# A two-layer backbone in split float32: weight splits, transposes and PSUM tiles where one sub-layer hands over to the next

## The chip, the cores and the metric

The kernel runs on one core of one Trainium2 chip, in one launch. The metric is the device time of one execution, in microseconds (us). TensorE (PE) multiplies and transposes, VectorE (DVE) and ScalarE (ACT) work element by element, SyncE (SP) issues the transfers; SBUF and PSUM are the core's two memories.

## The reference, cut to what matters

One inference step of two layers with shared weights over 256 tokens (128 of a prompt, group 0; 128 of a sample, group 1), model width 2048. Each layer is a token-mixing sub-layer and a feed-forward sub-layer:

```python
shift1, scale1, gate1, shift2, scale2, gate2 = _modulation(cvec, p['w_mod'], p['b_mod'])
h = _rmsnorm(x, p['g_pre_mix']) * (1 + scale1) + shift1
au, av, q, k, v, ga, gb = jnp.split(h @ p['w_in'], SPLITS, axis=-1)
...
merged = jax.nn.sigmoid(ga) * (ya @ p['w_pa']) + jax.nn.sigmoid(gb) * (_merge_heads(yb) @ p['w_pb'])
x = x + gate1 * _rmsnorm(merged @ p['w_out'], p['g_post_mix'])
h = _rmsnorm(x, p['g_pre_ffn']) * (1 + scale2) + shift2
f = jnp.square(jax.nn.relu(h @ p['w_ff1'])) @ p['w_ff2']
x = x + gate2 * _rmsnorm(f, p['g_post_ffn'])
```

What matters here is the end of a sub-layer: the norm of a row of the output needs the whole row, the sum `x + gate * norm` needs that norm, the next norm needs the whole new row, and only then can the next sub-layer's projection of that token begin.

## The kernel before

**Precision.** Every projection is done as three matmuls on pairs of high and low parts, `high*high + high*low + low*high`. A weight tile `raw` (128 x 1024, 512 KB, one transfer) is split by `split`: ACT copies it to the rounded `wh`, DVE subtracts `wl = raw - wh`. Activations are split in the same way into two tiles (`hi`, `lo`, which the rows call `u`). There are 928 weight tiles.

**Order.** The program is written out by hand, instruction by instruction, and each engine runs its own instructions strictly in that order, waiting at each for what it needs. A list of items (weight tiles and small steps) is walked at the end of `body`; before each weight tile `advance` fetches, copies and subtracts as many further tiles as counters allow: `cap` limits how many split tiles may stand ready and not yet be used up, 4 in ordinary stretches.

**The handover.** A pass is one column block of 512 outputs with its 8 weight tiles; a pass over rows with tokens as outputs (`tok`) can be cut in two half passes, one for each group of tokens. At the end of a sub-layer `lay_halves` does this with the last pass and with the first pass of the next sub-layer. So PE does, in this order, 8 places for group 0 of the last pass, 8 for group 1 of the last pass, 8 for group 0 of the next first pass, and 8 for group 1. They are called here p0 to p7, q0 to q7, r0 to r7 and s0 to s7; a place is the six matmuls of one weight tile for one group. The 8 weight tiles of the last pass are held over p and q, the 8 of the next over r and s. There are three such handovers: mixing to feed-forward, feed-forward to mixing, and mixing to feed-forward again.

While q runs, group 0's rows go through `chain`: sum of the squares, square root (ACT) and reciprocal (DVE), the four residual sums (DVE) with their squares (ACT, the tile `dump`), again root and reciprocal; then, for each quarter o of the row, a scaling (`scaled`, DVE), four transposes on PE into the PSUM tile `aux`, scale and shift (on DVE for o = 0 and 2, on ACT for o = 1 and 3), the copy to `hi` (ACT), and the subtraction to `lo` (DVE). Quarter o serves the tiles 2o and 2o+1 of r. While r runs, the same is done for group 1, for s. `step` puts the stages of the chain at places: the stages are called at the numbers in `CHAIN_AT`, and the four transposes are the stages at 6, 7, 9 and 11. For group 0 these are ahead of q6, q7, r1 and r3, for group 1 ahead of r6, r7, s1 and s3. They are called T1 to T8 here. In a handover to a feed-forward sub-layer a ninth set (`turn`) follows at s5.

`ahead(p)` sets `cap` at each place from q0 on: 10 splits less those used up, plus `AHEAD`. With the numbers of before, ten tiles (the 8 of the last pass and two of the next) are split until q7; the splitting of the third tile of the next pass is released at r1, and stands in the queues of ACT and DVE behind what group 1's chain has put there at r0 and r1. `split` puts copy and subtraction out together.

**PSUM.** The pool `psm` has two tiles of 128 x 1024 (two banks each). A pass takes one; the two half passes of a pass write the two halves of the same one (`G.ps` is given up after the second), and what reads the finished first half (`out_stats`, or `post` of the next pass) stands as a wait for the second half's first matmul, since waits go by tiles.

Of the kernel before, what the change touches and what calls it, by code (L numbers as in the profile page):

```python
# [22 lines left out]
SPLIT_BUFS = 4  # L23
# [21 lines left out]
S_STEP = 4  # L45
MOD_ON_PE = [n in PE_QUADS for n in range(48)]
LAST = [11, 4, 11, 4]
CHAIN_AT = (0, 1, 3, 4, 6, 7, 9, 11, 12)
AHEAD = [0] * 9 + [1, 2, 3, 4, 5, 6] + [6] * 6 + [7, 8, 9]
SWAP16 = [i ^ 16 for i in range(32)]  # L50


# [38 lines left out]
def body(tc, io):  # L91
# [14 lines left out]
    def u4(dt=F32, name="u4"):  # L106
        return u4p.tile([128, 1024], dt, tag="u4", name=name)
# [10 lines left out]
    def v4(t, n=4):  # L118
        return t.rearrange("p (b t) -> p b t", b=n)

    def f(t):
        return t.bitcast(F32)
# [169 lines left out]
        while flush and todo:  # L292
            finish()

    def split(job):
        wh, wl = v4(u4(F32R, "wh"), 2), v4(u4(F32R, "wl"), 2)
        r = v4(job.raw, 2)
        act(wh, r, AF.Copy)
        tt(wl, r, f(wh), op=OP.subtract)
        job.parts = (wh, wl)  # L300

    def mm_half(job, gs=(0, 1)):
# [457 lines left out]
    def chain(Y, hs, nxt, spill, g):  # L760

        def rms(st):
            s = tiny(1)
            dve.tensor_reduce(s, st, axis=AX.X, op=OP.add)
            return rms_cols(s)

        r = rms(Y["st"][g])
        yield
        st = tiny(4)
        for o in range(4):  # L770
            x = X[o][:, g, :]
            dve.scalar_tensor_tensor(x, Y["y"][o][:, g, :], r, x, op0=OP.mult, op1=OP.add)
            if nxt is None:
                nc.sync.dma_start(io["y"][:, o, g], x)
                continue
            act(dump, x, AF.Square, accum_out=st[:, o:o + 1])
            if spill is not None:
                nc.sync.dma_start(spill[:, o, g], x)
        if nxt is None:
            return  # L780
        yield
        r2 = rms(st)
        yield
        ln, ma, mb = nxt
        w = slice(128 * g, 128 * g + 128)
        xr = {}

        def scaled(o):
            if o < 4:
                xr[o] = s2()  # L790
                dve.tensor_scalar(xr[o], X[o][:, g, :], r2, None, op0=OP.mult)

        scaled(0)
        yield
        last = None
        for o in range(4):
            if g == 0:
                hs.append(quad())
            scaled(o + 1)
            ps = aux()  # L800
            x = xr.pop(o)
            for b in range(4):
                nc.tensor.transpose(ps[:, 128 * b:128 * b + 128], x[:, 128 * b:128 * b + 128], ident)
            if last is not None:
                tt(*last, op=OP.subtract)
            t, ps = v4(s2()), v4(ps)
            if o % 2 == 0:
                for m, src, op in ((ma, ps, OP.mult), (mb, t, OP.add)):
                    mat(ln, m, 4 * o, g), mat(ln, m, 4 * o + 3, g)
                    tt(t, src, mv[:, ln, m, 4 * o:4 * o + 4, g:g + 1].to_broadcast([128, 4, 128]), op=op)  # L810
            else:
                for b in range(4):
                    act(t[:, b, :], ps[:, b, :], AF.Identity, scale=mat(ln, ma, 4 * o + b, g),
                        bias=mat(ln, mb, 4 * o + b, g))
            hi, lo = (h[:, :, w] for h in hs[o])
            act(hi, t, AF.Copy)
            last = lo, t, f(hi)
            yield
        tt(*last, op=OP.subtract)

# [49 lines left out]

    def held(on):
        def go():
            P["held"], P["cap"] = on, HELD if on else SPLIT_BUFS
        return go

    def ahead(p):

        P["cap"] = HELD - max(0, p if p < 8 else 8 if p < 16 else p - 8) + AHEAD[p]

    chains = [[], []]  # L880

# [103 lines left out]
    for i in range(1, 5):  # L985
# [19 lines left out]
        def second(p, a=args):  # L1005
            def go():
# [6 lines left out]
        items.append(to_end(ENDS[i], 8 * (24 if i == 2 else 30), i))  # L1013
        lay(seqs[i][0][1:-LAST[i]])

    P = dict(held=False, nl=0, nm=0, ns=0, live=0, mlive=0, sp=0, cap=0, md=0, t=0, free=False, ml=0.0, t0=0, m0=0, rate=0.0, s0=S_START,
             s=[(g, slice(k, k + 1024)) for g in range(2) for k in (0, 1024)], end=8 * ENDS[0])

    def fetch(j, name):
# [4 lines left out]
    def advance():  # L1024
        while True:
            moved = False
            if P["nm"] < min(len(mloads), P["end"]) and P["mlive"] < MOD_BUFS + (START_BUFS if P["nm"] < 64 else 0):
                fetch(mloads[P["nm"]], "mraw")
                P["mlive"] += 1
                P["nm"] += 1  # L1030
                moved = True
            if P["nl"] < len(loads) and P["live"] < (RAW_HELD if P["held"] else RAW_BUFS) and loads[P["nl"]].after <= P["nm"]:
                fetch(loads[P["nl"]], "raw")
                P["nl"] += 1
                P["live"] += 1
                moved = True
            if P["ns"] < P["nl"] and P["sp"] < P["cap"]:
                split(loads[P["ns"]])
                P["ns"] += 1
                P["sp"] += 1  # L1040
                P["live"] -= 1
                moved = True
            if not moved:
                return
# [16 lines left out]
    for it in items:  # L1061
        if callable(it):
            if not P["free"]:
                advance()
            it()
        elif isinstance(it, int):
            for _ in range(it):
                advance()
                one_mod()
        else:  # L1070
            advance()
            job, gs, last = it
            pump(bgm)
            if max(load.values()) < BG_LIMIT:
                pump(bg)
            mm_half(job, gs)
            P["sp"] -= last
            P["t"] += len(gs) / 2 if job.group.tok else 1
            spread_s()
            if P["free"] and P["md"] < min(P["nm"], P["end"], quota()) and P["t"] - mods[P["md"]][0].after >= MOD_AGE:  # L1080
                if not mods[P["md"]][1]:
                    if load["dve"] < P["ml"]:
                        one_mod()
                elif P["md"] + 1 < P["nm"] and P["t"] - mods[P["md"] + 1][0].after >= MOD_AGE:
                    one_mod()
                    one_mod()
            ease(len(gs) / 2)
            G = job.group
            if G.part and job.kh in (0, 1, 3, 5, 7):
                if job.kh == 0:  # L1090
                    G.acc = u4()
                    act(G.acc, G.ps, AF.Copy)
                else:
                    tt(G.acc, G.acc, G.ps, op=OP.add)
                G.ps = None
                if job.kh == 7:
                    G.post(*((G.acc, gs) if G.tok else (G.acc,)))
                    G.acc = None
            elif job.kh == G.n - 1:
                G.post(*((G.ps, gs) if G.tok else (G.ps,)))  # L1100
                if last:
                    G.ps = None

    ms.__exit__(None, None, None)
    for p in reversed(pools):
# [90 lines left out]
```

## Time and profile before

| | us |
|---|---|
| median of three runs (2846.80 to 2850.64) | 2846.85 |
| the profiled execution | 2849.79 |
| its span, first to last instruction | 2848.0 |
| PE busy in the span | 2772.1 (97%) |
| DVE busy | 2030.6 (71%) |
| ACT busy | 1285.3 (45%) |
| bytes moved | 722.56 MB, 254 GB/s on average |

The profile is of one execution, whose span lies 1.79 us under its own time and 1.15 us above the median of the runs. A row of the order of time begins with its start (us from the span's start) and its length, then engine, line, operation and tiles; a number in brackets is the time its engine sat idle before it, and what ended that. A matmul's end is modelled and lies after the start of the next, so idle time in brackets is a little shorter than the distance that the waiting matmul was pushed. Line 78 is the helper through which ACT and DVE work is recorded; lines 316 to 318 are the three matmuls of a place, line 803 the transposes of the chain.

### The profile page before, as it was taken

Reading aid. Unit: us, or ns where it says so; the run is one execution under the profiler, and the core shown is the slowest. Engines: PE = TensorE matmul, PEld = TensorE weight load, DVE = VectorE, ACT = ScalarE, POOL = GpSimd, SP = SyncE. Lnnn points to the kernel's source line nnn. Section 1 sums busy time; section 2 is a strip of 40 time slices with the busy share of each in tenths; the row PEclk is TensorE's granted clock in tenths of the full one; section 3 lists DMA queues with packets and bytes.
Section 4 is the critical chain, followed back from the end, with each engine's and each line's share of the span. In section 5 each row is a group of like instructions: output and inputs, shape, how many; then the busy total and the mean of one; then the engine's idle time right before and its main releaser. Section 6 shows DMA issues by size and latency. Waiting matters only on the chain.

```text
span 2848.0 us, 41915 instructions
## 1 busy us (share of the span) xinstructions
PE 2772.1 (97%) x16510; PEld 2385.9 (84%) x16510; DVE 2030.6 (71%) x2568; ACT 1285.3 (45%) x1596; POOL 0.7 (0%) x6
## 2 busy tenths in 40 slices
PE   7999999999899999999989999999989999999998
PEld 5788777777798989989869987788769899898997
DVE  4655767777688898897757888688766556656555
ACT  4344554334444444444544436544445444444443
POOL 0000000000000000000000000000000000000000
PEclk9999999999899999999999999999999999999999
DMA  9978778876578678787748677777736565756663
GB/s 383 369 260 312 281 255 295 278 274 260 185 266 304 243 277 300 253 299 251 246 177 302 243 272 248 261 269 283 293 132 246 204 215 200 255 186 215 216 204 137
DMA packets 204822, 722.56 MB, mean 254 GB/s; under 512 B 22993, under 2 KB 25681, under 8 KB 204625
## 3 DMA queue, kind: packets, MB, share of 16 engines
q1 hardware_dynamic: 204624, 719.89, 70.7%
q8 instruction: 129, 2.11, 0.3%
q14 instruction: 69, 0.56, 0.1%
HBM read 713.42 MB, written 6.37 MB: 253 GB/s over the span
## 4 chain that ended last, share of the span: by engine, by line
PE 94%; ACT 2%; DVE 2%; DMA 1%; issue 0%; SPq 0%; DVEq 0%; ACTq 0%
PE mm L316 19%; PE mm L317 18%; PE mm L318 18%; PE mm L325 11%; PE mm L326 11%; PE mm L327 11%; PE aux L236 2%; DMA mraw<-wm 1%; DVE wl L78 1%; ACT u L78 1%; ACT wh L78 1%; ACT s L78 1%; DVE u L78 0%; ACT dump L78 0%; DVE s L78 0%
## 5 line engine op out<-in xcount | busy, mean ns | idle before, releaser
L78 DVE TENSOR_TENSOR wl<-raw,wh 128x1024 fp32r<-128x1024 f32 x928 | 1108.0, 1221 | 373.9 <-ACT wh L78 355.4
L78 ACT ACTIVATE wh<-raw 128x1024 fp32r<-128x1024 f32 x928 | 949.1, 1055 | 651.5 <-PE mm L317 150.1
L316 PE MATMUL mm<-wh,u 128*128 128x512 f32 x2368 | 942.4, 398 | 37.8 <-ACT wh L78 27.8
L317 PE MATMUL mm<-wl,u 128*128 128x512 f32 x2368 | 929.6, 393 | 5.8 <-DVE wl L78 5.8
L318 PE MATMUL mm<-wh,u 128*128 128x512 f32 x2368 | 928.5, 392 | 2.4 <-DVE u L78 2.4
L325 PE MATMUL mm<-u,wh 128*128 128x256 f32 x2688 | 763.2, 284 | 0.0
L326 PE MATMUL mm<-u,wh 128*128 128x256 f32 x2688 | 760.6, 283 | 0.0
L327 PE MATMUL mm<-u,wl 128*128 128x256 f32 x2688 | 760.6, 283 | 0.0
L316 PEld LDWEIGHTS mm<-wh,u 128*128 128x128 f32 x2368 | 448.4, 189 | 158.9 <-ACT wh L78 37.9
L317 PEld LDWEIGHTS mm<-wl,u 128*128 128x128 f32 x2368 | 448.7, 189 | 98.5 <-DVE wl L78 9.9
L318 PEld LDWEIGHTS mm<-wh,u 128*128 128x128 f32 x2368 | 448.2, 189 | 98.8 <-DVE u L78 3.8
L325 PEld LDWEIGHTS mm<-u,wh 128*128 128x128 f32 x2688 | 515.8, 192 | 13.8 <-issue 10.5
L326 PEld LDWEIGHTS mm<-u,wh 128*128 128x128 f32 x2688 | 515.9, 192 | 0.4
L327 PEld LDWEIGHTS mm<-u,wl 128*128 128x128 f32 x2688 | 515.8, 192 | 0.0
L78 DVE SCALAR_TENSOR_TENSOR mraw<-mraw,sbc 128x1024 f32<-128x1024 f32 x248 | 303.8, 1225 | 8.8
L78 DVE SCALAR_TENSOR_TENSOR junk<-mraw,sbc 128x1024 bf16<-128x1024 f32 x248 | 301.9, 1217 | 8.3 <-DMA mraw<-wm 8.3
L78 ACT ACTIVATE u<-mm 128x1024 f32<-128x1024 f32 (+1 forms) x83 | 76.6, 933 | 429.7 <-PE mm L327 277.9
L78 DVE TENSOR_TENSOR u<-u,u 128x1024 fp32r<-128x1024 f32 (+4 forms) x74 | 72.9, 992 | 207.4 <-ACT u L78 206.9
L78 DVE TENSOR_TENSOR u<-u,mm 128x1024 f32<-128x1024 f32 (+1 forms) x60 | 64.1, 1076 | 103.4 <-PE mm L318 67.1
L78 ACT ACTIVATE u<-u 128x1024 f32<-128x1024 f32 (+3 forms) x86 | 81.4, 949 | 32.4 <-DVE u L78 27.2
L236 PE MATMUL aux<-mraw,csw 128*32 128x512 f32 (+1 forms) x608 | 76.0, 585 | 15.7 <-DMA mraw<-wm 15.6
L78 ACT ACTIVATE u<-aux 128x512 fp32r<-128x512 f32 (+2 forms) x48 | 23.6, 492 | 114.4 <-PE aux L607 68.7
(97 smaller groups left out, 660.2 us busy)
## 6 DMA issues: line engine op xcount, KB each, us to landing
raw<-f SPq DMA_DIRECT2D x512, 512.0 KB, 4.2
mraw<-wm SPq DMA_DIRECT2D x384, 512.0 KB, 5.2
raw<-wi SPq DMA_DIRECT2D x288, 512.0 KB, 4.5
raw<-wo SPq DMA_DIRECT2D x64, 512.0 KB, 6.8
raw<-pa SPq DMA_DIRECT2D x32, 512.0 KB, 4.4
raw<-pb SPq DMA_DIRECT2D x32, 512.0 KB, 4.4
u<-gd SPq DMA_DIRECT2D x32, 256.0 KB, 5.5
u<-xT SPq DMA_DIRECT2D x4, 512.0 KB, 5.7
```

Source lines behind the costliest of these rows:

```text
L78: return fn(out, *a, **k)
L236: nc.tensor.matmul(p[32 * c:32 * c + 32, :128 * nb], csw[:, kt, :], r[:, kt - k0, :], start=kt < 4, stop=kt > 11, skip_group_check=True, t ...
L316: nc.tensor.matmul(o, hh, wh[:, j, :], start=first, stop=False)
L317: nc.tensor.matmul(o, hh, wl[:, j, :], start=False, stop=False)
L318: nc.tensor.matmul(o, lo, wh[:, j, :], start=False, stop=last)
L325: nc.tensor.matmul(o, wh[:, j, s], hh, start=first and b % 2 == 0, stop=False, **kw)
L326: nc.tensor.matmul(o, wh[:, j, s], lo, start=False, stop=False, **kw)
L327: nc.tensor.matmul(o, wl[:, j, s], hh, start=False, stop=last, **kw)
```

## The change

Five edits, all at the handover.

1. `split` becomes `split_high` (the copy on ACT) and `split_low` (the subtraction on DVE), and `advance` releases them by two separate limits, `cap` and `low`. Outside the handover `low` is 99, so that a subtraction still follows its copy.
2. `AHEAD` holds a pair for each place, and the numbers differ: one more copy is released at q4, up to five more by r0; subtractions from q5 on, up to three more at q7.
3. The first transposes come one place sooner (5 in place of 6 in `CHAIN_AT`): T1 ahead of q5, T5 ahead of r5.
4. In the chain `scaled(o + 1)` is put out after the copy to `hi` and no longer ahead of the transposes of o, and for even o the subtraction to `lo` follows at once and not a stage later.
5. `G.ps` is given up after each half pass, so each takes its own PSUM tile, the two in turn.

```diff
-CHAIN_AT = (0, 1, 3, 4, 6, 7, 9, 11, 12)
-AHEAD = [0] * 9 + [1, 2, 3, 4, 5, 6] + [6] * 6 + [7, 8, 9]
+CHAIN_AT = (0, 1, 3, 4, 5, 7, 9, 11, 12)
+AHEAD = [(0, 0)] * 4 + [(1, 0), (2, 1), (3, 2), (3, 3), (5, 3), (5, 4), (5, 5), (5, 5)] + [(6, 6)] * 4 + [
+    (7, 7)] * 2 + [(8, 8)] * 2 + [(9, 9), (9, 9), (10, 10), (10, 10)]
...
-    def split(job):
-        wh, wl = v4(u4(F32R, "wh"), 2), v4(u4(F32R, "wl"), 2)
-        r = v4(job.raw, 2)
-        act(wh, r, AF.Copy)
-        tt(wl, r, f(wh), op=OP.subtract)
+    def split_high(job):
+        wh = v4(u4(F32R, "wh"), 2)
+        act(wh, v4(job.raw, 2), AF.Copy)
+        job.parts = (wh,)
+
+    def split_low(job):
+        wh, = job.parts
+        wl = v4(u4(F32R, "wl"), 2)
+        tt(wl, v4(job.raw, 2), f(wh), op=OP.subtract)
         job.parts = (wh, wl)
...
-            scaled(o + 1)
             ps = aux()
...
             act(hi, t, AF.Copy)
+            scaled(o + 1)
             last = lo, t, f(hi)
+            if o % 2 == 0:
+                tt(*last, op=OP.subtract)
+                last = None
             yield
...
-        P["cap"] = HELD - max(0, p if p < 8 else 8 if p < 16 else p - 8) + AHEAD[p]
+        own = HELD - max(0, p if p < 8 else 8 if p < 16 else p - 8)
+        P["cap"], P["low"] = own + AHEAD[p][0], own + AHEAD[p][1]
...
-            if P["ns"] < P["nl"] and P["sp"] < P["cap"]:
-                split(loads[P["ns"]])
+            if P["nh"] < P["nl"] and P["nh"] - P["done"] < P["cap"]:
+                split_high(loads[P["nh"]])
+                P["nh"] += 1
+                moved = True
+            if P["ns"] < P["nh"] and P["ns"] - P["done"] < P["low"]:
+                split_low(loads[P["ns"]])
                 P["ns"] += 1
-                P["sp"] += 1
...
                 G.post(*((G.ps, gs) if G.tok else (G.ps,)))
-                if last:
-                    G.ps = None
+                G.ps = None
```

ACT at the first handover, from group 0's second square root (ahead of T1) on, before. The tiles are `tiny` (a statistic), `u` and `s` (activations), `dump` (the squares), `wh` (a copied weight tile):

```order
L78 ACTIVATE tiny<-tiny,epsb 128x1
L78 ACTIVATE u_6106<-s_6115 128x4x128
L78 ACTIVATE s_6135<-aux,mv 128x128 x4
L78 ACTIVATE u_6125<-s_6135 128x4x128
L78 ACTIVATE dump,tiny<-mm 128x512
L78 ACTIVATE tiny<-tiny,epsb 128x1
L78 ACTIVATE u_6161<-s_6171 128x4x128
L78 ACTIVATE dump,tiny<-u_5620 128x512
L78 ACTIVATE dump,tiny<-u_5622 128x512
L78 ACTIVATE dump,tiny<-u_5624 128x512
L78 ACTIVATE dump,tiny<-u_5626 128x512
L78 ACTIVATE wh<-raw 128x1024 x2
```

The same place now:

```order
L79 ACTIVATE tiny<-tiny,epsb 128x1
L79 ACTIVATE wh<-raw 128x1024
L79 ACTIVATE u_6103<-s_6110 128x4x128
L79 ACTIVATE wh<-raw 128x1024 x2
L79 ACTIVATE s_6148<-aux,mv 128x128 x4
L79 ACTIVATE u_6141<-s_6148 128x4x128
L79 ACTIVATE dump,tiny<-mm 128x512
L79 ACTIVATE tiny<-tiny,epsb 128x1
L79 ACTIVATE wh<-raw 128x1024 x2
L79 ACTIVATE u_6184<-s_6192 128x4x128
L79 ACTIVATE dump,tiny<-u_5620 128x512
```

Five copies of weight tiles stand ahead of the squares of group 1's residual sums; none did.

DVE at the same handover, from group 0's fourth scaling on, before (`SCALAR_TENSOR_TENSOR` is group 1's residual sums):

```order
L78 TENSOR_SCALAR s_6163<-u_5626,tiny 128x512
L78 TENSOR_TENSOR u_6126<-s_6135,u_6125 128x4x128
L78 TENSOR_TENSOR s_6171<-aux,mv 128x512
L78 TENSOR_TENSOR s_6171<-s_6171,mv 128x512
L78 SCALAR_TENSOR_TENSOR u_5620<-u_5413,tiny,u_5620 128x512
L78 SCALAR_TENSOR_TENSOR u_5622<-u_5416,tiny,u_5622 128x512
L78 SCALAR_TENSOR_TENSOR u_5624<-u_5419,tiny,u_5624 128x512
L78 SCALAR_TENSOR_TENSOR u_5626<-u_5422,tiny,u_5626 128x512
L78 TENSOR_TENSOR wl<-raw,wh 128x1024 x2
L78 TENSOR_TENSOR u_6162<-s_6171,u_6161 128x4x128
L78 TENSOR_REDUCE tiny<-tiny 128x1
```

Now, from group 0's first `lo` on:

```order
L79 TENSOR_TENSOR u_6104<-s_6110,u_6103 128x4x128
L79 TENSOR_TENSOR wl<-raw,wh 128x1024 x2
L79 TENSOR_SCALAR s_6154<-u_5624,tiny 128x512
L79 TENSOR_TENSOR wl<-raw,wh 128x1024
L79 TENSOR_TENSOR u_5422<-mm,u_5422 128x512
L79 TENSOR_REDUCE tiny<-tiny 128x1
L79 RECIPROCAL tiny<-tiny 128x1
L79 TENSOR_TENSOR u_6142<-s_6148,u_6141 128x4x128
L79 TENSOR_TENSOR s_6192<-aux,mv 128x512
L79 TENSOR_TENSOR s_6192<-s_6192,mv 128x512
L79 TENSOR_SCALAR s_6196<-u_5626,tiny 128x512
L79 TENSOR_TENSOR u_6185<-s_6192,u_6184 128x4x128
```

Three subtractions of weight tiles now stand ahead of the reading of the last pass's second half (`u_5422<-mm`), with which group 1's chain begins; the second `lo` (`u_6142`) and the fourth scaling (`s_6196`) stand behind its first reciprocal.

PE where q begins, before and now, with the numbers of the tiles (`mm` is the PSUM tile, `wh`, `wl` the weight parts):

```order
L317 MATMUL mm_5998<-wl_5945,u4_5478 128x512
L318 MATMUL mm_5998<-wh_5944,u4_5479 128x512
L316 MATMUL mm_5998<-wh_5829,u4_4638 128x512
L317 MATMUL mm_5998<-wl_5830,u4_4638 128x512
L318 MATMUL mm_5998<-wh_5829,u4_4639 128x512
```

```order
L322 MATMUL mm_5998<-wl_5946,u4_5478 128x512
L323 MATMUL mm_5998<-wh_5944,u4_5479 128x512
L321 MATMUL mm_6054<-wh_5829,u4_4638 128x512
L322 MATMUL mm_6054<-wl_5831,u4_4638 128x512
L323 MATMUL mm_6054<-wh_5829,u4_4639 128x512
```

The second half pass writes a tile that nobody is reading any more.

## Rows read from the trace of the kernel before

**Rows 1.** Page, busy us, share of the span, instructions.

```profile
PE 2772.1 (97%) x16510; PEld 2385.9 (84%) x16510; DVE 2030.6 (71%) x2568; ACT 1285.3 (45%) x1596; POOL 0.7 (0%) x6
```

**Rows 2.** Waits of PE, whole span: total us, times, longest us.

```profile
PE mm L316 <- ACT wh L78: 27.8, 9, 6.7
PE mm L317 <- DVE wl L78: 5.8, 9, 0.8
PE mm L316 <- DVE tiny L78: 3.1, 2, 1.6
```

**Rows 3.** Order of time, PE, first handover (start, length, idle before and releaser).

```profile
702.32 0.39 PE L318 MATMUL mm<-wh,u 128*128 128x512 f32 x1
704.27 0.50 PE L316 MATMUL mm<-wh,u 128*128 128x512 f32 x1 [1.56 <-DVE tiny L78]
...
712.59 0.60 PE L803 MATMUL aux<-ident,s 128*128 128x128 f32 x4
...
714.43 0.60 PE L803 MATMUL aux<-ident,s 128*128 128x128 f32 x4
...
726.31 0.79 PE L316 MATMUL mm<-wh,u 128*128 128x512 f32 x1 [6.70 <-ACT wh L78]
...
747.04 0.79 PE L316 MATMUL mm<-wh,u 128*128 128x512 f32 x1 [0.69 <-ACT s L78]
...
752.81 0.39 PE L316 MATMUL mm<-wh,u 128*128 128x512 f32 x1
...
761.93 0.28 PE L325 MATMUL mm<-u,wh 128*128 128x256 f32 x1
```

**Rows 4.** Order of time, PE, second and third handover and last pass.

```profile
1446.36 0.50 PE L316 MATMUL mm<-wh,u 128*128 128x512 f32 x1 [0.78 <-DVE u L78]
...
1490.05 0.50 PE L316 MATMUL mm<-wh,u 128*128 128x512 f32 x1 [1.29 <-ACT u L78]
...
1502.02 0.39 PE L316 MATMUL mm<-wh,u 128*128 128x512 f32 x1
...
2089.08 0.50 PE L316 MATMUL mm<-wh,u 128*128 128x512 f32 x1 [1.56 <-DVE tiny L78]
...
2144.23 0.28 PE L325 MATMUL mm<-u,wh 128*128 128x256 f32 x1
...
2828.66 0.50 PE L316 MATMUL mm<-wh,u 128*128 128x512 f32 x1 [0.78 <-DVE u L78]
```

**Rows 5.** Windows of 5 us: busy us of each engine, granted clock, DMA share.

```profile
745.00:750.00 5.00, 4.31 (x13) 2.81 (x12) 1.55 (x3) 1.58 (x3) 0.00 (x0) 0.55 0.30 108
1485.00:1490.00 5.00, 1.92 (x6) 1.05 (x6) 3.23 (x5) 4.93 (x9) 0.00 (x0) 1.00 0.29 104
2130.00:2135.00 5.00, 4.31 (x21) 3.25 (x20) 2.65 (x6) 1.64 (x3) 0.00 (x0) 1.00 0.45 147
```

**Rows 6.** Order of time, DVE, first handover.

```profile
709.92 0.88 DVE L78 TENSOR_SCALAR s<-u,tiny 128x512 f32<-128x512 f32 x2
...
721.49 2.73 DVE L78 SCALAR_TENSOR_TENSOR u<-u,tiny,u 128x512 f32<-128x512 f32 x4
726.29 2.36 DVE L78 TENSOR_TENSOR wl<-raw,wh 128x1024 fp32r<-128x1024 f32 x2 [2.07 <-ACT wh L78]
```

**Rows 7.** Order of time, ACT, first handover, and the table load of the second.

```profile
722.33 0.63 ACT L78 ACTIVATE dump<-u 128x512 bf16<-128x512 f32 x1
...
725.22 1.99 ACT L78 ACTIVATE wh<-raw 128x1024 fp32r<-128x1024 f32 x2
...
730.96 1.50 ACT L78 ACTIVATE s<-aux,mv 128x128 f32<-128x128 f32 x4 [3.76 <-PE aux L803]
...
1488.10 1.28 ACT L78 ACT_TABLE_LOAD   x1
1489.40 0.60 ACT L78 ACTIVATE u<-mm 128x512 f32<-128x512 f32 x1
```

**Rows 8.** Page, DMA issues: count, KB each, median us from issue to landing.

```profile
raw<-f SPq DMA_DIRECT2D x512, 512.0 KB, 4.2
```

More of the change, by code (lines that the diff above doesn't have):

```diff
@@ L872, in go @@
         def go():
-            P["held"], P["cap"] = on, HELD if on else SPLIT_BUFS
+            P["held"], P["cap"], P["low"] = on, HELD if on else SPLIT_BUFS, 99
         return go
     def ahead(p):
-        P["cap"] = HELD - max(0, p if p < 8 else 8 if p < 16 else p - 8) + AHEAD[p]
+        own = HELD - max(0, p if p < 8 else 8 if p < 16 else p - 8)
+        P["cap"], P["low"] = own + AHEAD[p][0], own + AHEAD[p][1]
     chains = [[], []]
@@ L1014, in body @@
         lay(seqs[i][0][1:-LAST[i]])
-    P = dict(held=False, nl=0, nm=0, ns=0, live=0, mlive=0, sp=0, cap=0, md=0, t=0, free=False, ml=0.0, t0=0, m0=0, rate=0.0, s0=S_START,
+    P = dict(held=False, nh=0, done=0, low=99, nl=0, nm=0, ns=0, live=0, mlive=0, cap=0, md=0, t=0, free=False, ml=0.0, t0=0, m0=0, rate=0.0, s0=S_START,
              s=[(g, slice(k, k + 1024)) for g in range(2) for k in (0, 1024)], end=8 * ENDS[0])
@@ L1076, in body @@
             mm_half(job, gs)
-            P["sp"] -= last
+            P["done"] += last
             P["t"] += len(gs) / 2 if job.group.tok else 1
```

## The prediction

> **What bounds the kernel now.** I read the busy shares of the page first: PE is busy for 2772.1 of 2848.0 us [rows 1], so nothing counts that does not shorten PE's own stream, and at most 76 us of idle time are there. The view of waits says what PE waits for [rows 2]: 27.8 us in nine waits for a copied weight tile, 5.8 us in nine for its subtraction, 3.1 us in two for the release of a PSUM tile. The order of time puts nearly all of this into the three handovers. At the first, q0 waits 1.56 us, r2 6.70 us, s0 0.69 us [rows 3], with shorter ones between. Outside the handovers PE runs without a gap that this change touches, so what is gained there stays gained.
>
> How much a handover loses. At full clock six places (q0 to q5) take 712.59 - 704.27 = 8.32 us, 1.39 each, and a place with transposes 714.43 - 712.59 = 1.84 us [rows 3]. The first handover begins when q0 could have begun, one sixth of a place after 702.32, at 702.55, and ends with the first matmul of the next whole pass at 761.93: 59.4 us. A wait of 1.56 us in brackets pushes q0 by 1.72, one of 0.78 by 0.94 (the modelled end hides 0.16). So the second runs from 1445.42 to 1502.02, 56.6 us, the third from 2087.36 to 2144.23, 56.9 us [rows 4]. The work in them is 24 places, nine of them with transposes (eight in the second): 15 x 1.39 + 9 x 1.84 = 37.4 us, or 37.0. They lose 22.0, 19.6 and 19.5, together **61.1 us**. About two thirds is waiting; the rest is a lower clock after it: s0 to s1 take 752.81 - 747.04 = 5.77 us where 1.39 + 1.84 = 3.23 are due, while the window around them shows a granted clock of 0.55 [rows 3, 5], which is the lower level (1.2 GHz) for most of it. One such slow stretch costs **2.5 us**.
>
> **The change part by part**, placed at the first handover with the lengths of before. No instruction is added or removed. The two PSUM tiles are both free in time, since the built order leaves q0 waiting only for a reader that ended long before, and r0, s0 and the next whole pass for none of PSUM; so the pushes at q0 and at s0 vanish, also the 0.94 at the start of the last pass [rows 4], where nothing else changes.
>
> *T1, one place sooner.* PE reaches q5 at 702.55 + 5 x 1.39 = 709.5, but group 0's first scaling, the first of two of 0.44, starts at 709.92 [rows 6] and is done at 710.4: a new wait of **0.9**. So the freed PSUM tile is half given back. Nobody is hurt behind it: the next six places have their tiles.
>
> *Copies and subtractions ahead of the chain.* DVE from T1's landing (0.60 later, 711.0): two adds of 0.69, a scaling 0.44, `lo` 0.69, two subtractions 2.36, a scaling, a subtraction 1.18 [rows 6], until 717.5. (The second scaling, now behind the adds, is done at 712.9, and T2 is due at 713.6.) ACT meanwhile: `hi` 0.55 (estimate: half the width of a copy, which takes 1.0 [rows 7]), two copies, four scalings 1.5, `hi`, and the square of q's result (0.75) until 717.8. This work is hidden behind q5 to r1, which PE leaves at 710.4 + 1.84 + 1.39 + 1.84 + 1.39 + 1.84 = 718.7. Then the reading of q's sum, root and reciprocal take to 719.0 and the second `lo` to 719.7, while r2's third matmul, which needs it, is due at 719.2: a wait of **0.6** in place of 6.70. Two adds and a scaling make T4's input ready at 721.5; PE is there at 720.7: **0.8**. The next two copies sit in ACT's idle time there; their transfers are gated by place q1 and land 4.2 us later [rows 8], about 710, against a need at 718.8.
>
> *What is late next: T5.* PE has done r4 at 724.7. T5 needs group 1's whole chain: third `lo` until 722.3, residual sums 2.73 (their first square starts 0.84 after the first sum, and four squares take 725.22 - 722.33 = 2.9 [rows 6, 7]) so until 726.0, the scalings of quarter 3 on ACT 1.5, `hi` 0.55, root and reciprocal 0.5, `lo` 0.6, scaling 0.44: 729.6. That is a wait of **4.9**, the old big wait's successor. A slow stretch behind it is to be expected, as behind the 6.70: **2.5**.
>
> *The end of s.* Counted from T6's landing, ACT does scalings 1.5, `hi` 0.55, the two steps of r's result 1.1, a copy 1.0; DVE then a subtraction 1.18 and `lo` 0.69: 6.0 us, plus 0.6 for the transposes. PE has 1.84 + 1.39 + 1.84 + 0.46 = 5.5 until s2's third matmul: **1.1**; T8 behind it **0.8**.
>
> Sum: 0.9 + 0.6 + 0.8 + 4.9 + 2.5 + 1.1 + 0.8 = 11.6 us lost where 22.0 and 19.5 were. The second handover has one more add of 0.69 ahead of group 1's root, and a table load and one step in place of two at r's result: 1.28 us [rows 7] plus 0.55 against 1.1, so 0.7 more; 13.0 us. Its residual rows also go to memory, and fetches for the next whole pass queue on SP behind those stores; they are needed only some 20 us later. Lost afterwards: 11.6 + 13.0 + 11.6 = 36.2; gained 61.1 - 36.2 + 0.9 = **25.8 us**.
>
> On the table load: the row after it starts 0.02 us behind its end [rows 7]. The Trainium skill (ScalarE: Activation LUTs, What ACT_TABLE_LOAD costs) counts a drain of about 1.38 us on top of the 1.28. By it the second handover would lose 1.4 us more and the gain would be 24.4; the row shows no such drain, so I leave it out.
>
> *The clock at s2 and T8* is the one price that before does not settle. Waits of like size stood ahead of s0 at all three handovers. The windows there show a granted clock of 0.55 once and 1.00 twice [rows 5]. Bounds: none or three slow stretches, 0 to 7.5 us. I take one of three, 2.5. The gain is then **23 us**. The profiled execution took 2849.79 us with a span of 2848.0, so it would take 2826.8; against the median of 2846.85 the same 23 us give **2824**.
>
> **The rivals.**
>
> *The clock stays low.* Each handover gets a slow stretch at s2, and the one behind T5 lasts twice as long: the gain falls from 25.8 to 18.3 (three at s2), or to 10.8 (both); 2829 to 2836. For it: several waits now lie near each other from T4 to T8. Against it: from T5 to s2 PE has ten microseconds without a wait. The Trainium skill (TensorE: Matmul & The Clock Gate, HAM oscillation — how this bites in real kernels) has every idle stretch that is long enough send the array back to the low clock, so that what follows a wait runs slowly too. By this rule, which speaks against leaving one wait of 4.9 us, T5 pays and the waits of 0.6 to 1.1 do not: 2821. The trace agrees about r2, whose first matmul after 6.70 us is 0.79 long in place of 0.39 [rows 3], and differs about s0 of the first handover.
>
> *The clock never falls*, since 4.9 us is less than 6.70: 25.8 + 7.5 = 33, 2814.
>
> *Group 1's chain is longer than placed.* It crosses between DVE and ACT at about twenty points from the second half's end to T5; 0.2 us more at each, or a copy of a weight tile that comes in ahead of a step, make T5's wait 4 us longer at each handover: 12 us, 2836; up to 2842. For it: ACT and DVE take their work strictly in order, and five copies and three subtractions were put ahead of it. Against it: the lengths are measured at this very place.
>
> *Slower: a weight tile that lands late.* The copies of tiles 5 and 6 now stand on ACT ahead of the third `hi` and the four squares. If one's transfer is late, ACT stands still, and with it group 1's chain and T5, microsecond for microsecond, three times over. The landing at about 710 leaves 9 us until 718.8; the change loses from there on when a landing comes some 8 us later than that (23 / 3), 17 us after it is due. Twelve us past the need would give 2846.85 - 23 + 36 = 2860. Against it: 4.2 us is the median landing [rows 8], and the transfer engines are far from busy late in this handover (a share of 0.30 [rows 5]).
>
> *The early release is empty*, because the third to seventh tiles are not fetched by then: only the PSUM waits fall, less T1's new wait, some 5 us: 2842.
>
> **How the numbers follow.** Forecast (2817 to 2829, most likely 2824): 0.58. Clock stays low (2829 to 2836): 0.14. Clock never falls (2808 to 2817): 0.08. Longer chain (2832 to 2843): 0.12. Empty release (2841 to 2846): 0.03. Late tile (2845 to 2860): 0.05. About 0.2% of the time, 5.7 us, is what a measurement can tell from no change: faster means under 2841.2, slower over 2852.5. Faster: 0.58 + 0.14 + 0.08 + 0.09 = 0.89; the same: 0.03 + 0.03 + 0.01 = 0.07; slower 0.04. The range 2814 to 2836 leaves out half of the fast case, nearly half of the longer chain and the last two, 0.18 in all.
>
> **What would show it.** In the order of time of the changed kernel: q0, r0 and s0 start without a wait; T1 stands ahead of q5 after a wait of about 0.9; r2 waits for a `lo` (DVE) under 1.5 us and for no copy; the longest wait, 4 to 6 us, is at T5, for the scaling on DVE; each handover is 46 to 51 us long. PE's total for waits on copies falls from 27.8 to near nothing. The forecast is wrong if ACT is seen waiting for a transfer within r, if T5's wait is above 8 us or missing, or if slow stretches stand at places other than r5, r6 and s2 to s4.

## The result and the profile after

The changed kernel takes 2824.8 us (median of six runs, 2822.88 to 2826.12), the kernel before in the same session 2849.77: a ratio of 0.9914, with a 95% interval of 0.9901 to 0.9927. The forecast was 2824, in a range of 2814 to 2836, reckoned from 2846.85, the median of the first three of the six runs of the kernel before. The profiled execution took 2825.56 us with a span of 2823.8.

First the busy line of the page, which answers to [rows 1], then the two largest waits of PE at the handovers (total us, times, longest us), which answer to [rows 2]. In the changed kernel line 79 is the helper of ACT and DVE, lines 321 to 323 are the three matmuls of a place, line 807 the transposes of the chain.

```profile
PE 2762.8 (98%) x16510; PEld 2381.8 (84%) x16510; DVE 2030.3 (72%) x2568; ACT 1284.7 (45%) x1596; POOL 0.7 (0%) x6
```

```profile
PE aux L807 <- DVE s L79: 20.7, 12, 4.8
...
PE mm L323 <- DVE u L79: 7.4, 8, 1.9
```

No matmul of the handovers waits for a weight tile any more. What waits now are the transposes, for a scaled quarter `s`, and the third matmul of a place, for a `lo`; both come from DVE. In order of time, PE, the first handover from q0 to the first matmul of the next whole pass (as [rows 3]):

```profile
703.74 0.39 PE L321 MATMUL mm<-wh,u 128*128 128x512 f32 x1
...
711.75 0.30 PE L807 MATMUL aux<-ident,s 128*128 128x128 f32 x1 [1.05 <-DVE s L79]
...
720.98 0.50 PE L323 MATMUL mm<-wh,u 128*128 128x512 f32 x1 [0.35 <-DVE u L79]
...
722.80 0.30 PE L807 MATMUL aux<-ident,s 128*128 128x128 f32 x1 [0.62 <-DVE s L79]
...
730.95 0.66 PE L807 MATMUL aux<-ident,s 128*128 128x128 f32 x2 [4.76 <-DVE s L79]
...
736.77 0.38 PE L807 MATMUL aux<-ident,s 128*128 128x128 f32 x2
...
743.59 0.50 PE L323 MATMUL mm<-wh,u 128*128 128x512 f32 x1 [1.16 <-DVE u L79]
...
745.32 0.33 PE L807 MATMUL aux<-ident,s 128*128 128x128 f32 x1 [0.53 <-DVE s L79]
...
753.02 0.36 PE L330 MATMUL mm<-u,wh 128*128 128x256 f32 x1
```

The rows with a bracket are T1, r2, T4, T5, s2 and T8, in this order; 736.77 is T6. The handover is 49.28 us long. The second and the third (as [rows 4]) show the first row, T5, s2 and the last row:

```profile
1436.59 0.39 PE L321 MATMUL mm<-wh,u 128*128 128x512 f32 x1
...
1464.15 0.44 PE L807 MATMUL aux<-ident,s 128*128 128x128 f32 x1 [4.85 <-DVE s L79]
...
1476.29 0.50 PE L323 MATMUL mm<-wh,u 128*128 128x512 f32 x1 [1.93 <-DVE u L79]
...
1486.59 0.39 PE L321 MATMUL mm<-wh,u 128*128 128x512 f32 x1
...
2070.87 0.39 PE L321 MATMUL mm<-wh,u 128*128 128x512 f32 x1
...
2098.38 0.38 PE L807 MATMUL aux<-ident,s 128*128 128x128 f32 x1 [4.79 <-DVE s L79]
...
2110.01 0.50 PE L323 MATMUL mm<-wh,u 128*128 128x512 f32 x1 [1.17 <-DVE u L79]
...
2121.01 0.36 PE L330 MATMUL mm<-u,wh 128*128 128x256 f32 x1
```

They are 50.0 and 50.1 us long. The work in a handover is 37.4, 37.0 and 37.4 us as before, so 11.9, 13.0 and 12.7 us are lost where 61.1 us were lost together: 23.5 us saved. With the 0.94 us at the last pass, which is gone, that is 24.4 us; the two profiled executions are 2849.79 - 2825.56 = 24.2 us apart. The whole result is in the handovers.

Windows of the changed kernel in the columns of [rows 5]; the granted clock is the figure behind the five busy times:

```profile
730.00:735.00 5.00, 4.05 (x12) 3.39 (x13) 4.53 (x8) 1.21 (x2) 0.00 (x0) 0.50 0.01 5
735.00:740.00 5.00, 5.00 (x23) 3.96 (x22) 0.28 (x1) 2.56 (x6) 0.00 (x0) 0.85 0.01 3
...
1475.00:1480.00 5.00, 3.28 (x11) 2.47 (x12) 4.41 (x7) 2.40 (x5) 0.00 (x0) 0.72 0.98 364
2110.00:2115.00 5.00, 4.46 (x15) 3.35 (x16) 3.59 (x6) 3.65 (x8) 0.00 (x0) 0.71 1.01 391
```

The first two stand behind T5 of the first handover; the last two are s2 to s4 of the second and of the third, where the clock falls a second time.

### The profile page after: what moved, and what is told of

Same layout as the page of the kernel before. It is cut to its first block, busy times and chain, and to the rows that moved or that the text cites. A ratio compares the mean times of both kernels' runs of the same rounds, so it can differ in the third digit from the quotient of the medians.

```text
span 2823.8 us, 41925 instructions
## 1 busy us (share of the span) xinstructions
PE 2762.8 (98%) x16510; PEld 2381.8 (84%) x16510; DVE 2030.3 (72%) x2568; ACT 1284.7 (45%) x1596; POOL 0.7 (0%) x6
## 4 chain that ended last, share of the span: by engine, by line
PE 93%; ACT 3%; DVE 2%; DMA 1%; issue 1%; SPq 0%; DVEq 0%; ACTq 0%
PE mm L321 18%; PE mm L322 18%; PE mm L323 18%; PE mm L330 12%; PE mm L331 11%; PE mm L332 11%; PE aux L237 2%; DMA mraw<-wm 1%; DVE u L79 1%; ACT dump L79 1%; DVE wl L79 1%; ACT u L79 1%; ACT s L79 1%; DVE s L79 1%; ACT wh L79 1%
## 5 line engine op out<-in xcount | busy, mean ns | idle before, releaser
L79 ACT ACTIVATE u<-aux 128x512 fp32r<-128x512 f32 (+2 forms) x48 | 23.5, 490 | 123.8 <-PE aux L612 68.8
```

Source lines behind the costliest of these rows:

```text
L79: return fn(out, *a, **k)
```

## The experiments

Eleven kernels were run. Edits are numbered as in the section on the change. "Handovers" is the sum of the three, from q0 to the next whole pass, in the profiled execution; a wait at q0 counts with the idle time in its bracket, so the kernel before has 172.4 (172.9 as the prediction reckons, with the whole push). It was timed again beside each group of kernels, at 2851.07 (the first four), 2850.09 (the next four) and 2849.66 us (the last three), so medians of different groups compare to about 1.5 us.

| kernel | median us | ratio to before, 95% | handovers us |
|---|---|---|---|
| all five edits | 2824.8 | 0.9901 to 0.9927 | 149.4 |
| edit 5 alone | 2838.23 | 0.9944 to 0.9971 | 161.3 |
| edits 1, 2, 3, 4 | 2824.91 | 0.9897 to 0.9924 | 147.0 |
| edits 1, 2, 4, 5 | 2817.30 | 0.9871 to 0.9898 | 142.0 |
| edits 1, 2 | 2825.82 | 0.9901 to 0.9928 | 148.8 |
| all five, T5's wait filled | 2817.13 | 0.9870 to 0.9897 | 142.6 |
| edits 1, 2, 4 | 2821.16 | 0.9885 to 0.9912 | 144.0 |
| edits 1, 2, 5 | 2819.88 | 0.9875 to 0.9905 | 143.9 |
| edits 1, 2, 4, 5, subtractions on GpSimd | 2828.43 | 0.9911 to 0.9936 | 154.3 |
| all five, one limit | 2834.18 | 0.9932 to 0.9957 | 159.6 |
| edits 1, 2, 4, 5, T5's wait filled | 2817.62 | 0.9872 to 0.9899 | 142.4 |
| edits 3, 4, 5 | 2845.33 | 0.9972 to 0.9990 | 170.0 |

The theory behind them is the prediction's: the long waits were for copies and subtractions queued behind the chain, and what is left is the chain itself, on DVE and ACT, with a slow clock behind T5. The rivals: the PSUM tiles or the earlier transposes bring the gain, or the chain is not what T5 waits for.

### The tiles alone, and the tiles taken away

Edit 5 alone:

```diff
-                if last:
-                    G.ps = None
+                G.ps = None
```

> The kernel before with the fifth edit alone: each half pass gets a PSUM tile of its own, the order of copies, subtractions and transposes stays. Theory of the prediction: the waits at q0 (1.72 us in handovers 1 and 3) and the idle 0.94 us before the last pass's second half at the kernel's end go, the wait at s0 (0.69, 1.29, 0.69 us) goes too; the ten other waits of a handover stay as they were. That is 2 x 1.72 + 0.94 + 2.7 = about 7 us: 2842 to 2844 us, handovers of about 57, 55 and 54 us. Rival 1: the work that waited at q0 and s0 only waits at the next place, the first transpose of the chain, since DVE and ACT have no less to do: 1 to 2 us in all, 2848 to 2849 us. Rival 2: DVE's and ACT's reads of the one tile and TensorE's writes to the other now collide and the half passes get slower: 2850 us or more.

It took 12.8 us off, more than the 7 expected. The waits at q0, at s0 and at the end are gone, which add up to 2 x 1.72 + 2 x 0.94 + 2.7 = 8 us. Of the rest, 2.5 us are the slow stretch that the prediction priced: in the kernel before, the wait at s0 of the first handover was followed by a granted clock of 0.55 [rows 5]; without the wait the window of the same time shows 1.00. Another 1.4 us are shorter waits for copies at r4: 0.99, 0.85 and 1.16 us, where the kernel before has 1.50, 1.89 and 1.05.

```profile
745.00:750.00 5.00, 4.60 (x22) 3.85 (x23) 3.66 (x7) 2.35 (x5) 0.00 (x0) 1.00 0.51 170
```

The opposite, edit 5 taken out of the changed kernel (the same lines the other way):

> The changed kernel with the fifth edit undone: both halves of a pass share one PSUM tile again. Theory of the prediction: TensorE waits again at q0 (1.7 us in two handovers), at s0 (0.7 to 1.3 us in three) and 0.94 us at the end, but the wait at the first transpose of the chain (1.05, 0.62, 1.34 us) lies behind q0's on the same chain of work and goes with it: net 3 to 6 us over the changed kernel, 2828 to 2831 us. Rival 1: the shared tile is the main thing in the change, then 8 us or more come back, 2833 us and above. Rival 2: the tile does not matter once copies and transposes come early: within 1.5 us of the changed kernel.

Nothing: 2824.91 against 2824.8 us. Rival 2 holds. PE waits 1.56, 0.78 and 1.56 us at q0 again and 1.34, 2.77 and 1.34 us at s0, but T1 no longer waits, in the second handover T5 waits 3.25 us in place of 4.85, and s2 waits in none of the three. With the early transposes the tile only moves waits along the chain.

### The early transposes taken away

```diff
-CHAIN_AT = (0, 1, 3, 4, 5, 7, 9, 11, 12)
+CHAIN_AT = (0, 1, 3, 4, 6, 7, 9, 11, 12)
```

> The changed kernel with the third edit undone: the first and the fifth transposes of the chain stand one place (1.39 us of matmuls) later again, ahead of q6, s6 and r6, s6. Theory A: what T1 and T5 wait for ends at the same time as before, so 1.39 us of matmuls slide under each of these waits: T1's wait (1.05, 0.62, 1.34 us) is gone and T5's falls from 4.8 to about 3.4 us, while T2 and T6 wait up to 0.6 us more because the next transposes lie only one place behind: 1 to 1.7 us a handover, 2820 to 2822 us. Rival B: the chain is the bound from q5 on and every place that T1 and T5 stand later comes back later by the same amount, as a longer wait at T4 and T8 and at the handover's end: within 1 us of the changed kernel. Rival C: TensorE's granted clock, which in the changed kernel is 0.50 in the stretch behind T5, falls less behind a shorter wait, and the handover gains 2.5 us more: 2813 to 2816 us.

2817.3 us: 7.5 us **faster** than the changed kernel, about twice what theory A expected and not as far as rival C. Order of time, PE, first handover, the rows of r5's second matmul, T5 and T6:

```profile
728.29 0.50 PE L322 MATMUL mm<-wl,u 128*128 128x512 f32 x1 [1.07 <-DVE wl L79]
...
731.77 0.45 PE L807 MATMUL aux<-ident,s 128*128 128x128 f32 x1 [2.05 <-DVE s L79]
...
735.21 0.41 PE L807 MATMUL aux<-ident,s 128*128 128x128 f32 x1
```

T5 starts 26.9 us behind q0 here (704.86) and 27.2 in the changed kernel: the chain ends when it ends, wherever PE waits for it. But here r5's six matmuls are done before the wait, at full clock; in the changed kernel they stand behind it, in the slow stretch. So T6 follows T5 after 3.44 us and not 5.82; in the second and third handovers after 2.78 and 2.95 and not 4.56 and 4.82 (in the second the clock stayed at 1.00 there). T6 thus comes 2.7, 2.2 and 2.2 us sooner behind q0, 7.1 of the 7.4 us by which the handovers differ. Where, as here, the input comes at the same time whatever the place of the transpose, the transpose should stand as late as its users allow, since each place that it stands sooner moves six matmuls behind the wait.

### The early release alone, and the other edits beside it

Edits 1 and 2 alone (edits 3, 4 and 5 undone):

> The first and second edits alone: copies and subtractions of the weight splits are released separately, by position; transposes, the order of scaling and rounding and the PSUM tiles as in the kernel before. Theory of the prediction: these two edits carry the two long waits of a handover, at the fourth and the fifth transposes, and with them most of the 15 us of slow clock that no later wait repeats: 10 to 16 us of the 25, 2834 to 2840 us. Rival 1: without the early rounding of the even blocks and without tiles of their own the freed time on ACT and DVE is not used by the chain, 0 to 5 us: 2845 to 2850 us. Rival 2: the release is all of it, 2825 to 2829 us.

Rival 2 holds: 25 us, as much as all five edits, because edits 4 and 5 win what edit 3 loses. The two runs between tell edits 4 and 5 apart. Beside edits 1 and 2, edit 4:

```diff
-            scaled(o + 1)
             ps = aux()
...
             act(hi, t, AF.Copy)
+            scaled(o + 1)
             last = lo, t, f(hi)
+            if o % 2 == 0:
+                tt(*last, op=OP.subtract)
+                last = None
```

> Edits 1, 2 and 4 (split release, early rounding of the even blocks), with the transposes and the shared PSUM tile as in the kernel before. Edits 1 and 2 alone took 2825.8 us, edits 1, 2, 4 and 5 took 2817.3. Theory A: edit 4 brings the share that it was forecast to bring, since with edits 1 and 2 alone TensorE waits 3.4 us in r5 for an unrounded remainder, the third lo: that wait becomes a wait of 2 us at T5, 1 to 1.4 us a handover, 2821 to 2823 us; the rest is edit 5's. Theory B: edit 5 brings nothing beside edits 1, 2 and 4, as beside all the others (2824.9 against 2824.8): 2816 to 2819 us.

And edit 5 beside edits 1 and 2:

> Edits 1, 2 and 5 (split release, a PSUM tile for each half pass), with transposes and rounding as in the kernel before. Theory A: the waits at q0 (1.56, 0.78, 1.84 us), s0 (1.5, 2.8, 1.5 us) and at the end (0.94) of the kernel with edits 1 and 2 alone go, and about half of that comes back as waits at the second transposes and in s2: 5 to 6 us, 2819 to 2821 us. Theory B: all of it comes back on the chain, since the transposes stand behind the same work of DVE and ACT: 2824 to 2826 us, less the 0.94 at the end.

Theory A holds in both: 4.7 us for edit 4, 5.9 for edit 5, and 8.5 for the two together (2817.3), a little less than the sum. The first two figures are rough: the four runs of edits 1 and 2 alone took 2823.1, 2823.6, 2828.0 and 2828.8 us. With edits 1 and 2 alone the longest wait of a handover is not at T5 but in r4 (not in r5, as the expectation has it), for the third `lo`, 3.4 us: edit 4 moves this subtraction ahead of the residual sums. Edit 3 costs 3.7 us beside edits 1, 2 and 4, and 7.5 us beside 1, 2, 4 and 5.

Edits 3, 4 and 5 without the release:

```diff
-AHEAD = [(0, 0)] * 4 + [(1, 0), (2, 1), (3, 2), (3, 3), (5, 3), (5, 4), (5, 5), (5, 5)] + [(6, 6)] * 4 + [
-    (7, 7)] * 2 + [(8, 8)] * 2 + [(9, 9), (9, 9), (10, 10), (10, 10)]
+AHEAD = [(n, n) for n in [0] * 9 + [1, 2, 3, 4, 5, 6] + [6] * 6 + [7, 8, 9]]
```

> The changed kernel with edits 1 and 2 undone: copies and subtractions are released together and at the places of the kernel before; transposes one place sooner, early rounding and a PSUM tile for each half pass stay. Edit 5 alone took 2838.2 us, edits 1 and 2 alone 2825.8, all five 2824.8. Theory: without the early release the long waits for copies at r2 (6.7 us) and the ones for copies in s stay, and the three other edits bring what edit 5 brings alone, with early rounding 0 to 2 us a handover better and early transposes up to 2.6 us worse: 2836 to 2844 us. Rival: the gains do not add up but come from the early release alone once it is there, so that the other three are worth nothing in sum without it too: 2848 to 2851 us.

2845.33 us, 1 us outside the theory's range and short of the rival's: the wait for copies at r2 is even longer than before. Since edit 5 alone took 2838.2, edits 3 and 4 cost some 7 us here; the eleven runs of this kernel lie between 2839.3 and 2848.0 us, and the profiled one, whose handovers the table gives, is the longest of them. The row of r2's first matmul:

```profile
729.15 0.80 PE L320 MATMUL mm<-wh,u 128*128 128x512 f32 x1 [7.53 <-ACT wh L78]
```

### One limit for copies and subtractions

```diff
-        P["cap"], P["low"] = own + AHEAD[p][0], own + AHEAD[p][1]
+        P["cap"], P["low"] = own + AHEAD[p][0], own + AHEAD[p][0]
```

> The changed kernel with one limit for copies and subtractions (the larger one, that of the copies): the subtraction of a tile is released together with its copy, as in the kernel before, but as early as the copies of the changed kernel. Theory: two subtractions of 1.14 us more stand on VectorE ahead of the adds of T1 to T3 and of the second lo, so r2's wait (0.35, 1.10, 0.35 us) and T1's or T2's grow by 1 to 2 us; T5's wait shrinks by at most as much, since VectorE has the same work to do by then: 0 to 1.5 us a handover, 2825 to 2829 us. Rival 1: VectorE's idle spots (1.1 and 0.4 us in q5 to q7) take both subtractions in, and those ahead of the reduction that T5 waits for are fewer: T5's wait falls by 1 to 2 us, 2817 to 2822 us. Rival 2: no difference, 2823.5 to 2826 us.

Worse than any of the three: 9.4 us lost. In the first handover r2 now waits 3.27 us for its `lo` in place of 0.35. First DVE's two rows, then PE's row:

```profile
721.22 2.36 DVE L79 TENSOR_TENSOR wl<-raw,wh 128x1024 fp32r<-128x1024 f32 x2 [0.78 <-ACT wh L79]
723.49 0.68 DVE L79 TENSOR_TENSOR u<-s,u 128x512 fp32r<-128x512 f32 x1
```

```profile
724.23 0.50 PE L323 MATMUL mm<-wh,u 128*128 128x512 f32 x1 [3.27 <-DVE u L79]
```

A subtraction put out with its copy stands on DVE waiting for ACT, 0.78 us idle, and the second `lo` queues behind both of them, 3.14 us in all. That is what the separate limits of edit 1 are worth: copies may run ahead on ACT while DVE does the chain first.

### T5's wait filled

Eighteen matmuls whose result nobody reads, ahead of T5's transposes:

```diff
+            if g == 1 and o == 0:
+                d, h = aux(), hs[0][0]
+                for _ in range(18):
+                    nc.tensor.matmul(d, h[:, 0, 0:128], h[:, :, 0:128], start=True, stop=True)
             for b in range(4):
```

> The changed kernel with 18 matmuls of 512 columns added ahead of the fifth transposes of the chain, at all three handovers; their result goes into a tile that nobody reads. At 0.23 us each they fill 4.1 of the 4.8 us that TensorE waits there, so nothing else moves. Theory: what is slow behind this wait is the granted clock alone (0.50 in the stretch behind it). From T5 to T6 the changed kernel takes 5.82, 4.56 and 4.82 us where 12 matmuls and four transposes at full clock take 3.24, so 5.5 us come back: 2819 to 2820 us, with the clock at 1.00 from r5 on. If the second slow stretches, at s2 to s4 of the second and third handovers, are a consequence of the first ones, about 3 us more: 2816 to 2817 us. Rival: r5 and r6 are slow for another reason (their tiles or the DVE's work), then the 18 matmuls are only extra work in a wait: 2824 to 2826 us. Rival on the losing side: matmuls in the wait delay T5 itself, which then starts later: 2826 to 2830 us.

7.7 us faster than the changed kernel, with more work. PE's rows (17 of the 18 are in the trace) and the window behind T5, where the changed kernel has a clock of 0.50:

```profile
725.61 4.01 PE L807 MATMUL aux<-u 128*128 128x512 f32 x17
...
730.25 0.55 PE L811 MATMUL aux<-ident,s 128*128 128x128 f32 x3 [0.63 <-DVE s L79]
```

```profile
730.00:735.00 5.00, 4.75 (x25) 4.01 (x26) 4.10 (x7) 1.48 (x4) 0.00 (x0) 1.00 0.01 3
```

T5 starts as late as before (27.1 us behind q0, 27.2 in the changed kernel), so the chain is untouched. From T5 to T6 it takes 3.26, 3.26 and 3.24 us in place of 5.82, 4.56 and 4.82: 5.4 us, all clock. The slow stretches at s2 went from two to one: now the first handover has one (0.72 in 740 to 745) and the others none, though s2 waits there as long as before, 1.17, 1.93 and 1.17 us.

The same with eight matmuls in the kernel without edit 3:

> The kernel with edits 1, 2, 4 and 5 (transposes as before, 2817.3 us) with 8 matmuls of 512 columns added ahead of the fifth transposes, whose result goes into a tile that nobody reads: 1.84 us of the wait of 2.05 us there. Theory: the clock behind T5 stays at 1.00. From T5 to T6 that kernel takes 3.44, 2.78 and 2.95 us where six matmuls and four transposes at full clock take 1.85, so 3.6 us come back: 2813 to 2814 us; with the slow stretches at s2 gone in one or two handovers 2811 to 2812 us. Rival: the clock falls all the same, because of the wait of 1.07 us for a subtraction in r5, which stays unfilled: 2816 to 2818 us.

The rival's number, 2817.62 against 2817.3 us, but not its reason: the clock did stay at 1.00 behind T5, and the time did not move. T5 and T6 of the first handover:

```profile
729.97 0.33 PE L811 MATMUL aux<-ident,s 128*128 128x128 f32 x1
...
732.92 0.30 PE L811 MATMUL aux<-ident,s 128*128 128x128 f32 x1 [0.91 <-DVE s L79]
```

T6 now waits 0.91 us for the next scaling, which the slow clock had covered without the filling. So T6 comes 0.6 us sooner behind q0 in the first handover, and within 0.1 us as before in the others; and the clock fell at s2 in two handovers where it had fallen in one. The sums of the handovers, 142.4 and 142.0 us, are the same.

### The subtractions on another engine

In the kernel without edit 3, at the handovers only:

```diff
-        tt(wl, v4(job.raw, 2), f(wh), op=OP.subtract)
+        (nc.gpsimd.tensor_tensor if P["low"] < 99 else tt)(wl, v4(job.raw, 2), f(wh), op=OP.subtract)
```

> The kernel with edits 1, 2, 4 and 5 (transposes as before, 2817.3 us), and in the handovers the subtractions of the weight splits go to GpSimd, which has nothing to do there, in place of VectorE. Theory: VectorE's queue is what T2, T4 and T5 wait for. Two subtractions of 1.14 us stand ahead of the reduction that T5 hangs on; without them it can start when the fourth square is read, 1.2 us earlier, so T5's wait falls from 2.05 to under 1 us, r5's wait for a subtraction (1.07 us) goes, T2's (1.06 us) too: 2 to 3 us a handover, 2808 to 2812 us. Rival 1: a subtraction on GpSimd takes longer than TensorE needs for a place with the same tile (1.39 us); no row of any trace so far shows its length. Then r waits for it: at twice VectorE's time some 2 to 5 us a handover, 2823 to 2833 us. Rival 2: VectorE slows down while GpSimd works, so that what leaves its queue comes back as longer instructions: 2816 to 2819 us.

11.1 us slower than that kernel. The time lies in the first rival's range, but its wait is not there: PE waits for no `wl` in the handovers, though a subtraction is longer than a place. The second rival's mechanism is there, at a higher price than it set: in the first handover T2 waits 3.6 us and T4 2.9, both for a scaling on DVE. Order of time, GpSimd and then DVE, at the end of q and the beginning of r of the first handover:

```profile
720.19 5.14 POOL L304 TENSOR_TENSOR wl<-raw,wh 128x1024 fp32r<-128x1024 f32 x2 [3.48 <-ACT wh L79]
```

```profile
720.08 0.69 DVE L79 TENSOR_TENSOR s<-aux,mv 128x512 f32<-128x512 f32 x1
720.80 2.33 DVE L79 TENSOR_TENSOR s<-s,mv 128x512 f32<-128x512 f32 x1
723.05 2.56 DVE L79 TENSOR_SCALAR s<-u,tiny 128x512 f32<-128x512 f32 x1
725.53 0.68 DVE L79 TENSOR_TENSOR u<-s,u 128x512 fp32r<-128x512 f32 x1
```

A subtraction takes 2.5 us on GpSimd (1.22 on DVE), and while two of them run, DVE's add of two SBUF tiles takes 2.33 us in place of 0.69 and its scaling 2.56 in place of 0.48. The freed queue was paid for by the instructions left in it. So this run doesn't tell what a shorter DVE queue would be worth.

## Why the prediction was right, and where it was not

**Step by step**, predicted and then measured at the three handovers, in us:

| step | predicted | first | second | third |
|---|---|---|---|---|
| q0, r0, s0, last pass | none | none | none | none |
| T1 | 0.9 | 1.05 | 0.62 | 1.34 |
| r2's `lo` | 0.6 (second 1.3) | 0.35 | 1.10 | 0.35 |
| T4 | 0.8 | 0.62 | 0.53 | 0.62 |
| T5 | 4.9 | 4.76 | 4.85 | 4.79 |
| slow clock behind T5 | 2.5 | 2.6 | 1.3 | 1.6 |
| s2 | 1.1 (second 1.8) | 1.16 | 1.93 | 1.17 |
| T8 | 0.8 | 0.53 | 0.43 | 0.53 |
| slow clock at s2 | one of three, 2.5 | 0 | 1.3 | 1.6 |

The slow stretches behind T5 are T6 - T5 less 3.24 (twelve matmuls and four transposes at full clock, as with the wait filled); those at s2 are the time from T8 to the end less what it takes at full clock: 7.70 us, as in the first handover, and 7.30 in the second, which has no ninth transposes (read there with the wait filled). The order of the waits, the places, the engine that ends each, and the lengths of the waits to 0.5 us are as forecast. That T5's wait came out within 0.15 us at all three handovers shows that its working held: the chain of group 1 through the third `lo`, the residual sums, the squares, ACT's scalings, root, reciprocal and scaling. Its last links on DVE, T5's input being the fourth row:

```profile
728.48 0.15 DVE L79 TENSOR_REDUCE tiny<-tiny 128x1 f32<-128x4 f32 x1
729.66 0.16 DVE L79 RECIPROCAL tiny<-tiny 128x1 f32<-128x1 f32 x1 [1.03 <-ACT tiny L79]
729.74 0.67 DVE L79 TENSOR_TENSOR u<-s,u 128x512 fp32r<-128x512 f32 x1
730.33 0.48 DVE L79 TENSOR_SCALAR s<-u,tiny 128x512 f32<-128x512 f32 x1
```

**Where the size was off.** The clock: one slow stretch was priced at 2.5 us, and four of them, 10 us, were expected. There were five, of 1.3 to 2.6 us, 8.3 us in all; the errors cancelled in part. Behind T5 of the second and third handovers a stretch cost 1.3 and 1.6 us in place of 2.5. The chance of one in three at s2 was read from three windows [rows 5], of which the second ends at 1490.00, just ahead of the s0 that it was to show (1490.05 [rows 4]); the next one, 1490 to 1495, has a clock of 1.00 too, so the reading stands.

**Where luck helped.** The gain was forecast at 23 us and is 25.0 by the medians. The forecast was reckoned from 2846.85 us, and the kernel before took 2849.77 beside the changed one. So the gain was 2 us too small and the base 2.9 us too low; that the number came within 0.8 us owes something to this.

**The table load.** In the second handover ACT's rows on the way to s2 are, as in [rows 7], without a drain:

```profile
1471.54 1.28 ACT L79 ACT_TABLE_LOAD   x1
1472.83 0.60 ACT L79 ACTIVATE u<-mm 128x512 f32<-128x512 f32 x1
```

s2 then waited 1.93 us where the row gave 1.8. The 1.38 us of drain that the Trainium skill (ScalarE: Activation LUTs, What ACT_TABLE_LOAD costs) adds would have made it 3.2; the measurement decides for the row.

**The rival on the clock.** "The clock never falls" did not come: it fell behind T5 at all three handovers. The rival set 7.5 us for the stretches behind T5; filling T5's wait gave back 5.4 there and 7.7 in all. "The clock stays low" was half right: s2 got a slow stretch at two handovers, but T5's did not last longer. The rule of the Trainium skill that was weighed there (TensorE: Matmul & The Clock Gate, HAM oscillation — how this bites in real kernels) would have had T5 pay and the short waits not. The trace agrees about T5 and differs about s2: a wait of 1.17 us, with one of 0.53 close behind it, was followed by a clock of 0.71 in the third handover and by 1.00 in the first.

**What the prediction left out.** It priced edit 3 only as T1's new wait of 0.9 us, half of what the freed PSUM tile gives. The runs show that this edit takes back all of edit 5's 3.9 us beside edits 1, 2 and 4, and costs 7.5 us in the whole. The paragraph on T5 passed this over: it took the wait of 4.9 us with the transposes where the change puts them, and the slow stretch as a fixed 2.5, without asking what T5 one place later would have given. The prediction came right because it added up the changed kernel's waits, and not the worth of each edit. For the same reason it took edit 5, less T1's wait, for some 5 us; alone it is worth 12.8, beside the four others nothing.

Which condition decides whether the clock falls stays open: with waits of the same length at s2 it fell in some handovers and not in others, and without edit 3 T5 waited 2.05, 2.05 and 2.04 us while the windows of 5 us with its start show 0.53, 1.00 and 0.66.

## What to carry to other kernels

Work that many later steps need (here copies of weights) is best released on the engine that has time, apart from the step that follows it on the engine that the critical chain uses: that alone was worth 25 us, and one limit for both gave 9.4 us of it back. Where PE has to wait for a chain, let it first do all that doesn't depend on it; what is moved behind the wait costs its time there, and may run at the low clock. Price a change by the sum of the waits that it leaves, but look at each edit against its undoing as well: the five edits together gave 25 us, four of them 34.

## What the runs showed of the hardware

- Filling a wait of 4.8 us with unused matmuls made the kernel 7.7 us faster; TensorE went on at a granted clock of 1.00 (2.4 GHz) where it had been 0.50 (1.2 GHz). Filling one of 2.05 us brought the clock back too, but no time, since the next wait of the chain took it.
- A DVE add of two SBUF tiles (0.69 us alone) took 2.33 us and a scaling (0.48 us alone) 2.56 us while GpSimd subtracted; the multiplication that reads PSUM (`aux`) kept its 0.69 us at 720.08, as did the subtraction at 725.53 (0.68), behind GpSimd's work. The Trainium skill (SBUF — State Buffer, SBUF: two separate sides) says that DVE and GpSimd share a pair of ports, which one of them holds for a whole instruction while the other stands still, and names DVE instructions with two SBUF inputs among those that need it. These rows agree: the add ended 0.6 us behind the start of GpSimd's second subtraction (722.54), and the scaling 0.3 us behind the end of it (725.33).
